# Mixing layer and first two up pairs issued from one list of single steps, residual stores on SyncE's queue, three gates of attention scaled from PSUM

## The chip, the cores and the metric

The kernel runs on one core of one Trainium2 chip. The time is in device microseconds, from runs of the whole program. The core has five engines with a queue each: TensorE (PE in the profile; PEld is its weight load), VectorE (DVE), ScalarE (ACT), GpSimd (POOL) and SyncE (SP). Matrix products go to PSUM, all else lies in SBUF or in device memory.

## What is computed

One decoder layer on 1024 tokens of width 1024, in float32, and a final norm. Cut to what matters here:

```python
xn = rmsnorm(x, norm_mix_w)
da_q, da_k, da_v, sw_q, sw_k, sw_v, g_da, g_sw = split_cols(xn @ w_in)
y_da = diff_attention(da_q, da_k, da_v, lam, lam_init, subln_w)
y_sw = sliding_window_attention(sw_q, sw_k, sw_v, sinks)
merged = sigmoid(g_da) * (y_da @ w_br_da) + sigmoid(g_sw) * (y_sw @ w_br_sw)
x = x + merged @ w_mix_out
xn = rmsnorm(x, norm_ffn_w)
u = xn @ w_up                     # 2 * 2816 columns: gate and value
c = causal_depthwise_conv3(u, conv_w, conv_b)
x = x + (silu(gate(c)) * value(c)) @ w_down
return rmsnorm(x, norm_final_w)
```

## The kernel before

**Layout and products.** Everything lies transposed: channels on the 128 partitions, tokens along the free axis, so a tile holds 128 channels of 1024 tokens, and a half (`hf`) 512 tokens. For precision every operand is split into a high part (a rounded copy, made on ACT) and a low part (what is left, made on DVE by a subtraction), and a product is three matmuls of 512 columns per 128 rows: high by high, high by low, low by high. Large products are done two blocks at a time by Strassen's scheme with seven block products (`P1` to `P7`) instead of eight, on sums and differences of operand halves. In names, `B11`, `B21`, `B22`, `T1`, `T3` (together `T13`), `T2`, `T4` (together `T42`; `N2` is `T2` with its sign turned) are activation operands, `A11`, `A12`, `A22`, `S1` to `S4` weight operands.

**Stages.** `project` makes queries, keys, values and gates; two blocks of columns make a pair (`self.pairs`), the last being the gates 21 and 22. The norm's factor `rstd` (one per token) is multiplied in after a product. A pair's two results `us` are multiplied by it on POOL (line 523); gates are stored to device memory (`gd`, line 525, on SP), the others go through `keep`. `attention` runs six units (four heads of differential attention, two groups of sliding windows). Between its steps `back_half` (line 635) does the products of the gates 23 to 33 by halves, as filler for TensorE, in the order of `HALVES`: ACT copies the half out of PSUM (line 642), unscaled, and ACT's queue stores it (643). The weights, the attention bias and the query and key stacks `u` are loaded on SP's queue.

**Gates before mixing.** `rest` runs over eight pairs of strips `m` in the order 0, 4, 1, 5, 2, 6, 3, 7. For each it loads the gate of both branches (line 878), multiplies it by `rstd` on POOL (line 881) where it was stored unscaled (branch 1 always; branch 0, gates 18 to 25, for m of 5, 6 and 7), takes the sigmoid on ACT (883), and multiplies on DVE with the branch products in PSUM (893, 900, 901). `mix_operands` makes the operands of the mixing layer from two merged strips (932 to 937).

**Mixing layer.** `mix` has 28 runs (`run`, slots 0 to 27), each of twelve matmuls, in two groups of 14 (G = 0 and 14) of two strips each. Two runs share a unit of weights: one load on SP, a cast `wh` on ACT (206) and a low part `wl` on DVE (208), held in two buffers. Runs of one strip accumulate in one PSUM bank; after each the bank is added on DVE to one half of the residual `X[m]` (`add`, line 1032), which frees it for the next run. When a half is complete, `post` takes its square on ACT (994) and adds that on POOL to the sum over channels (995), stores the half to device memory on ACT's queue (`x2d`, line 999), and for m > 3 multiplies it by the norm's weight (`norm_w`, 987) into another tile; for m < 4 that multiply overwrites the half in place, after the store has read it. From the normed strips come the operands of the up products by `cast` (ACT, 1008), `low` (DVE, 1017) and `diff` (DVE, 1024).

**Order.** Each step is entered as an event with a number, `at(16.02, add, ...)`; the events are sorted by it and issued in that order. `in_order` then ties every instruction of ACT, DVE and POOL to the one before it on its engine, so these three run in the listed order. TensorE's and SP's instructions are not tied: their order is made by the framework when the program is built, from the order of issue and its own estimate of when data are ready.

**Up products.** `hidden` does 22 pairs of blocks of `w_up`. Pair 0 is written out: the first three of four strips of five products, then the split of `T42`, then the fourth strip, the column sums (235) and the norm's factor (`power` on POOL, 244), then `P6` and `P4`. Its results are combined on DVE, while pair 1 is prepared: weight sums on POOL (`sums`), casts and low parts. Then the first two products of pair 1 and the `spread` of the factor over the partitions (250). `steady` does the pairs from 1 on.

Of the kernel before, what the change touches and what calls it, by code (L numbers as in the profile page):

```python
# [26 lines left out]
RAW = 3  # L27
HP, HPB, HR = 7, 13, 11
# [13 lines left out]
NVEC = C_LAM + 256  # L42


class Trunk:
# [286 lines left out]
    def project(self):  # L332
# [6 lines left out]
        with ExitStack() as ctx:  # L339
# [171 lines left out]
            for j, ms in enumerate(self.pairs):  # L511
# [10 lines left out]
                for m, u in zip(ms, us):  # L522
                    nc.gpsimd.tensor_tensor(u, u, self.rstd, ALU.mult)  # L523
                    if self.kind[m] == "g":
                        nc.sync.dma_start(self.gd[m - 18], u)
                    else:
                        self.keep(m, u, (tp, "hi"))
# [100 lines left out]
    def store(self, dst, src):  # L628

        self.stores.append((dst, src))  # L630
# [5 lines left out]
    def back_half(self, m, hf):  # L636
# [5 lines left out]
        self.nc.scalar.copy(g, ps)  # L642
# [200 lines left out]
    def rest(self, gctx):  # L843
        nc, tc = self.nc, self.tc
        with ExitStack() as ctx:
            e = ctx.enter_context
            actx, mctx, gctx3 = ExitStack(), ExitStack(), ExitStack()
            with gctx, ExitStack() as bctx:
# [22 lines left out]
                for m in self.mix_order:  # L871
# [4 lines left out]
                    for br in range(2):  # L876
# [3 lines left out]
                        if br or m > 4:  # L880
# [64 lines left out]
    def mix(self, ga, gb, mctx, gctx3):  # L945
# [40 lines left out]
        def norm_w(m, hf):  # L986
            nc.scalar.mul(h2(t42[m - 4] if m > 3 else X[m], hf), h2(X[m], hf), self.vecs[:, C_NF + m:C_NF + m + 1])

        def post(m, hf):

            x = h2(X[m], hf)
            if hf in begun:
                sq = self.tl(stp, [P, H2], "s")
                nc.scalar.activation(sq, x, AF.Square)  # L994
                gt(h2(acc, hf), h2(acc, hf), sq, ALU.add)  # L995
            else:
                nc.scalar.activation(h2(acc, hf), x, AF.Square)
# [5 lines left out]
        events = []  # L1003
        at = lambda p, f, *a, **k: events.append((p, len(events), lambda: f(*a, **k)))
# [14 lines left out]
        def put(p, q, name, k, t):  # L1019
            at(p, cast, name, k, t)  # L1020
            at(q, low, name, k, t)
# [4 lines left out]
        def run(slot, bank, name, first):  # L1026
            if slot % 2 == 0:
                self.unit = self.wq.pop(0)
            self.product(bank(), [t[:, slot % 2 * 4:slot % 2 * 4 + 4] for t in self.unit], name, first=first, skip=True)
# [24 lines left out]
        for G, a in ((0, 0), (14, 2)):  # L1054
            for d in range(2):
# [3 lines left out]
                for slot, n, name, fresh in ((2 * d, n1, "B11", True), (2 * d + 1, n2, "B21", True), (2 * d + 4, n1, "T2", False),  # L1059
                                             (2 * d + 5, n3, "T1", True), (2 * d + 8, n1, "T3", False), (2 * d + 9, n3, "B22", False),  # L1060
                                             (d + 12, n1, "T4", False)):
                    at(G + slot, run, slot, (lambda n=n, x=x: new(n, (n, x))) if fresh else old(n), name, fresh)
                for slot, m, hf, n, sign in ((0, x, 0, n1, ALU.add), (1, x, 0, n2, ALU.add), (4, x, 1, n1, ALU.add), (5, x + 4, 1, n3, ALU.subtract),
                                             (8, x + 4, 1, n1, ALU.subtract), (9, x, 1, n3, ALU.add), (12, x + 4, 0, n1, ALU.subtract)):
                    p = G + slot + (d if slot == 12 else 2 * d) + 1.02
                    at(p, add, m, hf, old(n), sign)
                    if slot in (1, 8, 9, 12):
                        if slot == 8:
                            at(p, tile42, x)
                        at(p + (.28 if p > 28 else .43), post, m, hf)  # L1070
                    if slot == 1:
                        at(p + 1.88, norm_w, x, 0)
                    if slot == 9:
                        at(p + (1.6 if x == 3 else 1.7 if x == 2 else 1.88), norm_w, x, 1)
            for u in range(7):
                if G + 2 * u < 26:
                    at(G + 2 * u + .05, self.ahead, 1)
        at(-.9, load, 0)
        at(-.8, load, 4)
        at(-.7, load, 1)  # L1080
        at(-.6, load, 5)
        at(-.5, load, 2)
        at(13.3, load, 3)
        at(14.3, load, 6)
        at(15.3, load, 7)
        part = lambda *names: lambda: self.mix_operands(3, *names, ga=ga, gb=gb)
        at(-.4, part("B11", "B21"))
        at(.5, part("B22", "T13"))
        at(1.6, part("N2", "T4"))
        put(3.95, 4.4, "B11", 0, xh(0, 0))  # L1090
        put(9.6, 10.1, "B22", 0, th(0, 1))
# [625 lines left out]
```

## Time and profile before

| | us |
|---|---|
| median of three runs | 1336.41 |
| lowest and highest | 1334.08, 1336.58 |
| the profiled execution, its own time | 1336.43 |
| its span, from the first to the last instruction | 1334.5 |

The profile is that of one execution. Times in it count from the first instruction. A view by stretches gives the busy time of each engine between two times, with the clock that TensorE was granted (1.00 is full) and the share of the DMA engines. A list of waits says which instruction of an engine waited for which other, in total, how often and longest. In a timeline a row has start, duration, engine, line of the kernel, operation, output and inputs by the program's names, shapes, count and, in brackets, the idle time before it with what ended it. `n` and `bank` are PSUM banks of the mixing and up products, `g`, `sc` and `t` those of gates, scores and transposes; `m...` and `B_0`, `T_0` are operands, `x` the residual strips, `c` and `t` the strips of `T42`.

### The profile page before, as it was taken

What the parts mean: (1) busy time and instruction counts of PE and PEld (TensorE: products, weight loads), DVE (VectorE), ACT (ScalarE), POOL (GpSimd) and SP (SyncE); (2) the same over time, 40 slices, a digit from 0 to 9 for tenths busy, and PEclk for the clock granted to TensorE, in tenths of its full rate; (3) what the DMA queues carried; (4) which work ended last, traced back from release to release, by engine and by line L of the source; (5) the groups of instructions that cost most, each with busy time, mean ns of one, the idle gap of its engine ahead of it and who ended that gap; (6) DMA issues with size and microseconds to landing.
All of it is one profiled execution on the core that took longest, in us unless ns stands there. A gap on an engine that the chain in (4) does not pass through costs nothing.

```text
span 1334.5 us, 17079 instructions
## 1 busy us (share of the span) xinstructions
PE 1306.9 (98%) x6162; PEld 1085.0 (81%) x6162; DVE 1061.7 (80%) x1458; ACT 670.2 (50%) x1071; POOL 466.0 (35%) x371
## 2 busy tenths in 40 slices
PE   9999999999999999999989999999999999999997
PEld 7888888788888878777777888888888888888886
DVE  8866674288888976986868988888988898896865
ACT  8422232267667766334455454545454544554543
POOL 0448675100111003311226676657666632000002
PEclk9999999999999999999989999999999999999999
DMA  8256786876544236344533537745655249833534
GB/s 290 96 200 168 228 228 193 251 194 175 143 131 139 94 114 243 124 152 157 182 127 119 181 129 177 165 168 127 198 144 125 73 138 311 304 99 116 166 97 146
DMA packets 79332, 220.64 MB, mean 165 GB/s; under 512 B 8848, under 2 KB 16656, under 8 KB 79120
## 3 DMA queue, kind: packets, MB, share of 16 engines
q1 hardware_dynamic: 61760, 186.52, 42.6%
q0 software_dynamic: 4608, 15.73, 7.3%
q10 hardware_dynamic: 12880, 17.31, 3.7%
q8 instruction: 48, 0.79, 0.3%
q14 instruction: 36, 0.29, 0.1%
HBM read 169.72 MB, written 81.26 MB: 188 GB/s over the span
## 4 chain that ended last, share of the span: by engine, by line
PE 77%; DVE 9%; issue 4%; ACT 4%; DMA 3%; POOL 2%; SPq 1%; POOLq 0%; ACTq 0%; DVEq 0%
PE n L1157 30%; PE y L1530 9%; PE t L1157 9%; PE d L1530 7%; PE g L227 3%; PE g L228 3%; PE g L229 3%; PE sc L713 3%; PE t L729 1%; PE t L832 1%; PE sc L801 1%; DVE wl L208 1%; DMA yr<-gd 1%; PE t L741 1%; PE t L822 1%
## 5 line engine op out<-in xcount | busy, mean ns | idle before, releaser
L1460 POOL TENSOR_TENSOR us<-us,rstd 128x1024 f32<-128x1024 f32 x42 | 105.2, 2506 | 146.6 <-DVE us L1374 110.8
L208 DVE TENSOR_TENSOR wl<-raw,wh 128x1024 fp32r<-128x1024 f32 (+2 forms) x91 | 95.4, 1049 | 47.5 <-ACT wh L206 39.2
L206 ACT CAST wh<-raw 128x1024 fp32r<-128x1024 f32 (+2 forms) x91 | 80.4, 884 | 87.1 <-PE y L1530 47.5
L157 DVE TENSOR_TENSOR sl<-sf,sh 128x1024 fp32r<-128x1024 f32 x44 | 107.6, 2447 | 3.9 <-ACT sh L150 3.9
L244 POOL TENSOR_TENSOR rs<-ms,mhalf 128x8 f32<-128x8 f32 (+2 forms) x9 | 13.3, 1474 | 247.4 <-DVE ms L242 241.2
L1386 DVE SCALAR_TENSOR_TENSOR c<-us,vecs,c 128x1024 f32<-128x1024 f32 x76 | 95.6, 1279 | 0.7
L1530 PE MATMUL y<-h,wh 128*128 128x512 f32 (+1 forms) x324 | 95.2, 377 | 0.0
L1530 PE MATMUL d<-h,wh 128*128 128x512 f32 x264 | 81.3, 389 | 0.0
L227 PE MATMUL g<-xh,wh 128*128 128x512 f32 x176 | 71.5, 406 | 1.5 <-ACT g L642 1.5
L228 PE MATMUL g<-xl,wh 128*128 128x512 f32 x176 | 70.8, 402 | 0.0
L229 PE MATMUL g<-xh,wl 128*128 128x512 f32 x176 | 70.8, 402 | 0.0
L1530 PEld LDWEIGHTS y<-h,wh 128*128 128x128 f32 x324 | 59.4, 188 | 11.1
L717 DVE CUSTOM_DVE_ANT_0 L<-sc,bias 128x128 f32<-128x128 f32 (+7 forms) x64 | 47.7, 751 | 21.6 <-PE sc L713 18.4
L718 ACT ACTIVATE L<-L,sm 128x128 f32<-128x128 f32 (+7 forms) x64 | 49.6, 778 | 24.7 <-DVE sm L717 22.0
L1530 PE MATMUL y<-h,wl 128*128 128x512 f32 (+1 forms) x162 | 60.9, 376 | 0.0
L523 POOL TENSOR_TENSOR us<-us,rstd 128x1024 f32<-128x1024 f32 x18 | 52.2, 2905 | 17.3 <-DVE us L546 15.6
L1530 PEld LDWEIGHTS d<-h,wh 128*128 128x128 f32 x264 | 49.6, 188 | 10.3
L995 POOL TENSOR_TENSOR rstd<-rstd,s 128x512 f32<-128x512 f32 x14 | 21.5, 1539 | 91.7 <-ACT s L994 91.7
L713 PE MATMUL sc<-u,u 128*128 128x512 f32 (+2 forms) x192 | 50.0, 360 | 3.2 <-DMA u<-qd 3.0
L696 POOL MEMSET aT<- 128x128 f32 x32 | 6.1, 204 | 132.5 <-PE t L742 96.0
L157 DVE TENSOR_TENSOR wl<-raw,wh 128x1024 fp32r<-128x1024 f32 (+1 forms) x23 | 27.6, 1201 | 30.4 <-ACT wh L150 30.4
L1530 PE MATMUL d<-h,wl 128*128 128x512 f32 x132 | 51.5, 390 | 0.0
(747 smaller groups left out, 4252.0 us busy)
## 6 DMA issues: line engine op xcount, KB each, us to landing
u<-qd SPq DMA_DIRECT2D x72, 256.0 KB, 6.9
raw<-in_w_up SPq DMA_DIRECT2D x24, 512.0 KB, 3.9
raw<-in_w_in SPq DMA_DIRECT2D x22, 512.0 KB, 5.6
rv<-in_w_up SPq DMA_DIRECT2D x22, 512.0 KB, 3.5
hd<-c SPq DMA_DIRECT2D x22, 512.0 KB, 5.4
sdP<-in_w_down POOLq DMA_DIRECT2D x16, 704.0 KB, 8.5
qd<-us SPq DMA_DIRECT2D x15, 512.0 KB, 3.8
raw<-sdP SPq DMA_DIRECT2D x16, 384.0 KB, 3.0
```

What stands on the lines that cost most here:

```text
L157: self.nc.vector.tensor_tensor(lo, src, hi.bitcast(F32), ALU.subtract)
L206: self.hi = nc.scalar.copy(wh, raw)
L208: self.lo = (eng or nc.vector).tensor_tensor(wl, raw, wh.bitcast(F32), ALU.subtract)
L227: nc.tensor.matmul(ps, wh[:, kc + o, :], ah, start=first and n == 0, stop=False)
L228: nc.tensor.matmul(ps, wh[:, kc + o, :], al, start=False, stop=False)
L229: nc.tensor.matmul(ps, wl[:, kc + o, :], ah, start=False, stop=last and n == len(kcs) - 1)
L523: nc.gpsimd.tensor_tensor(u, u, self.rstd, ALU.mult)
L713: nc.tensor.matmul(sc[:, lo + n0:lo + n1], qs, k[c][part][:, n0:n1], start=part == 0, stop=part == 1)
L1157: nc.tensor.matmul(ps, (ah, ah, al)[p][:, k, :], (bh, bl, bh)[p], start=first and n == p == 0, stop=last and p == 2 and n == len(ks) - 1, ...
L1386: nc.vector.scalar_tensor_tensor(c, us[:, 2 - n:T + 2 - n], cw[2 - n], c, ALU.mult, ALU.add)
L1460: i = (nc.vector if m % NF == 0 else nc.gpsimd).tensor_tensor(us[:, 2:], us[:, 2:], self.rstd, ALU.mult)
L1530: nc.tensor.matmul(ps, v[:, k - k0, :], x, start=start and k == i == 0, stop=k == HK - 1 and i == 2, skip_group_check=True)
```

## The change

The sorted events of `mix` and the hand-written start of `hidden` give way to two lists of named steps (`STEPS`), issued in the order in which they stand, again under `in_order`. A name's first letters say what it is: `l` load of a strip of x, `C` and `O` cast and low part of a mixing operand of strip 3, `S` the sums of operand halves between them, `r` a run, `a` an add, `wc` and `wl` cast and low part of a unit of weights, `q` the square, `s` the store, `n` the norm's weight, `c` and `o` cast and low part of an up operand, `d` a difference, `raw` a load of weights, `sa` and `sb` weight sums, `P` products of the up pairs with their part, `sp` and `csp` the spread and the copy of it. What `post` did in one is now three steps, and the store is on SP's queue. The spread comes after the first two products of pair 1, not before the first of them is ready.

Gates 21 and 22 leave `project` unscaled. `LATE` names the gates that are scaled in `rest`: these two (m of 3 and 4 in branch 0) and all of branch 1. The gates 23, 24 and 25 are scaled in `back_half`, on DVE, as they leave PSUM.

```diff
+LATE = (21, 22, *range(26, 34))
+STEPS = (
+    """
+    l5 CB11 OB11 CB21 OB21 S1 banks l4 l0 r0 r1 S2 wc1 wl1 CT13 OT13 r2 l2 CB22 OB22 a0 S3 CN2 a1 r3 wc2 l1 wl2 ON2 S4 a2 a3 s0_0 r4 a4 r5 wc3 wl3 wc4
+    q0_0 n0_0 r6 wl4 r7 wc5 q1_0 r8 a5 a8 s1_0 CT4 wl5 a6 OT4 a7 r9 a9 s0_1 r10 q4_1 q0_1 cB11_0 oB11_0 r11 wc6 wl6 wc7 a10 n0_1 wl7 n4_1 d1_0 cB22_0 r12
+    a11 q5_1 q1_1 oB22_0 s5_1 d2_0 cT13_0 r13 a13 wc8 n1_0 a12 wl8 r14 r15 r16 s1_1 n4_0 cB21_0 n5_0 oT13_0 d3_0 n5_1 s4_1 oB21_0 s5_0 q4_0 q5_0 a14 a15
+    wc9 wl9 cB11_1 oB11_1 n1_1 r17 q2_0 s2_0 d4_0 n2_0 wc10 l3 raw0_sb r18 d1_1 d2_1 cT3_1 wl10 s4_0 cB21_1 a16 a17 oT3_1 cB22_1 oB22_1 d3_1 r19 a18 wc11
+    wl11 r20 a20 cB11_2 l6 r21 cT1_1 q3_0 oB21_1 wc12 d4_1 s3_0 n3_0 cB11_3 r22 oT1_1 oB11_2 l7 a19 a21 a22 q6_1 r23 oB11_3 wl12 n6_1 cB22_2 a23 s2_1 wc13
+    wl13 r24 a24 r25 raw0 q2_1 n2_1 d1_2 q7_1 r26 a25 s7_1 s3_1 d2_2 oB22_2 s6_1 cg_0 og_0 cT13_2 q3_1 a26 oT13_2 n7_1 cB22_3 r27 q6_0 raw0_sa n6_0 cB21_2
+    n3_1 s6_0 a27 n7_0 oB21_2 q7_0 d3_2 oB22_3 s7_0
+    """,
+    """
+    csa_0 cB21_3 osa_0 csb_0 osb_0 d1_3 d4_2 d2_3 cT42_1 oB21_3 d3_3 d4_3 oT42_1 places cT13_3 cT42_3 P1_0 P2_0 cT42_2 P5_0 P7_0 oT13_3 oT42_3 P3_0 cT42_0
+    oT42_0 cv_0 oT42_2 outs P1_1 P2_1 P5_1 P7_1 raw1 P3_1 sums P6_0 mean cg_1 og_1 ov_0 P4_0 results s1 u2 u4 u3 power sa1 csa_1 osa_1 c11 c12 c22 places2
+    sb1 raw2 P1_2 sa2 P2_2 sp0 sp1 csb_1 osb_1 cv_1 ov_1 csp0 csp1 c21
+    """,
+)
...
                 for m, u in zip(ms, us):
-                    nc.gpsimd.tensor_tensor(u, u, self.rstd, ALU.mult)
+                    if m < 21:
+                        nc.gpsimd.tensor_tensor(u, u, self.rstd, ALU.mult)
...
-        self.nc.scalar.copy(g, ps)
+        if m in LATE:
+            self.nc.scalar.copy(g, ps)
+        else:
+            self.nc.vector.tensor_tensor(g, ps, self.rstd[:, hf * H2:(hf + 1) * H2], ALU.mult)
...
-                        if br or m > 4:
+                        if 18 + 8 * br + m in LATE:
                             i = nc.gpsimd.tensor_tensor(g, g, self.rstd, ALU.mult)
...
-            nc.scalar.dma_start(self.x2d[m, :, hf * H2:(hf + 1) * H2], x)
-            if m > 3:
-                norm_w(m, hf)
...
+        def store(m, hf):
+            nc.sync.dma_start(self.x2d[m, :, hf * H2:(hf + 1) * H2], h2(X[m], hf))
...
+        def at(name, f, *a, **k):
+            assert name not in step
+            step[name] = lambda: f(*a, **k)
+
+        def weights():
+            src, nk, *more = self.wsrc.pop(0)
+            raw = more[2] if more else self.load_raw(src, nk)
+            wh, wl = (self.tl(self.wp, [P, nk, P], t, F32R) for t in ("wh", "wl"))
+            nc.scalar.copy(wh, raw)
+            self.wq.append((wh, wl, raw))
+
+        def weights_low():
+            wh, wl, raw = self.wq[-1]
+            tt(wl, raw, wh.bitcast(F32), ALU.subtract)
+            self.ahead(0)
...
+                for m in (x, x + 4):
+                    at(f"l{m}", load, m)
+                    for hf in range(2):
+                        at(f"q{m}_{hf}", square, m, hf)
+                        at(f"s{m}_{hf}", store, m, hf)
+                        at(f"n{m}_{hf}", norm_w, m, hf)
...
         with self.in_order(self.last):
-            gone = False
-            for p, n, f in sorted(events, key=lambda e: e[:2]):
...
+            self.steps(0)
...
+    def steps(self, n):
+        for name in STEPS[n].split():
+            self.step.pop(name)()
...
+                    with self.in_order(self.last):
+                        self.steps(1)
```

More of the change, by code (lines that the diff above doesn't have):

```diff
@@ L1075, in mix @@
[L1075 to L1089, printed above, removed]
@@ new lines, in mix, with banks @@
+        at("raw0", fetch_pair)
+        for key in ("sa", "sb"):
+            at(f"raw0_{key}", fetch_sums, key)
+        for key in ("g", "sa", "sb", "v"):
+            at(f"c{key}_0", self.cast, pair, key)
+            at(f"o{key}_0", self.low, pair, key)
+        def banks():
+            gctx3.close()
+            self.pctx.close()
+            self.first = ExitStack()
+            self.psF = self.first.enter_context(tc.tile_pool(name="psE", bufs=1, space=PSUM, reuse_waits="tile"))
+        at("banks", banks)
@@ L1168, in hidden @@
                      ("P3", "S4", "B22"), ("P6", "S2", "T2"), ("P4", "A22", "T4"))
-            more = self.ends
-            for p, key in ((28.04, "sa"), (28.5, "sb"), (29, "v")):
-                more.append((p, len(more), lambda key=key: self.whole(pair, key)))
-            with self.in_order(self.last):
-                for p, n, f in sorted(more, key=lambda e: e[:2]):
-                    f()
             w0 = pair["w"]
@@ new lines, in hidden @@
+                    x42, tt, v = {}, nc.vector.tensor_tensor, {}
+                    at("places", places)
+                    for n, (name, a, b) in enumerate(prods):
+                        ks = ((0, range(3)), (1, (3,))) if n < 5 else ((0, range(4)),)
+                        for part, k in ks:
+                            at(f"{name}_{part}", lambda name=name, a=a, b=b, k=k, part=part, n=n:
+                               self.product(ps[name], w[a], b, k, first=not part, last=bool(part) or n > 4))
@@ new lines, in hidden @@
+                    for n, (a, b) in enumerate((("A11", "B11"), ("A12", "B21"))):
+                        at(f"P{n + 1}_2", lambda n=n, a=a, b=b: self.product(v["b"][n], st[1]["w"][a], b, skip=True))
+                    for hf in range(2):
+                        at(f"sp{hf}", lambda hf=hf: self.spread(v["sps"][hf], v["rs"], hf * 4))
+                        at(f"csp{hf}", lambda hf=hf: nc.scalar.copy(self.rstd[:, hf * H2:(hf + 1) * H2], v["sps"][hf]))
+                    with self.in_order(self.last):
+                        self.steps(1)
+                        assert not self.step, list(self.step)
```

242 lines of the change are left out of this document (111 added, 131 removed).

## The prediction, made before the run

> **What bounds the kernel now.** I read the page first, for the share of each engine, then the busy time by stretches, which gives the granted clock, then the list of waits of TensorE.
>
> ```profile
> span 1334.5 us, 17079 instructions
> PE 1306.9 (98%) x6162; PEld 1085.0 (81%) x6162; DVE 1061.7 (80%) x1458; ACT 670.2 (50%) x1071; POOL 466.0 (35%) x371
> ```
>
> TensorE is busy for 98% of the span, and the change removes no matmul. So it can only win what TensorE loses between matmuls, or by running some of them slowly. The stretches say where that is; the columns after the length are busy us and instructions of PE, weight load, DVE, ACT and POOL, then the granted clock.
>
> ```profile
> core 0: us, PE busy (x) PEld busy (x) DVE busy (x) ACT busy (x) POOL busy (x), PEclk, DMA share, GB/s
> 800.00:820.00 20.00, 20.00 (x90) 16.56 (x89) 16.70 (x12) 10.42 (x14) 13.33 (x10) 1.00 0.67 158
> 254.00:262.00 8.00, 5.03 (x17) 3.86 (x16) 0.00 (x0) 0.25 (x1) 0.00 (x0) 0.79 1.04 276
> 262.00:480.00 218.00, 216.55 (x1337) 187.34 (x1336) 190.23 (x557) 152.71 (x384) 18.78 (x63) 1.00 0.52 144
> 565.00:573.00 8.00, 5.59 (x24) 3.99 (x23) 7.24 (x10) 2.53 (x3) 2.80 (x1) 1.00 0.44 140
> 606.00:613.00 7.00, 4.78 (x20) 3.27 (x20) 5.00 (x7) 3.71 (x6) 0.00 (x0) 1.00 0.21 74
> 659.00:667.00 8.00, 6.22 (x19) 4.07 (x18) 6.66 (x11) 1.94 (x3) 0.00 (x0) 0.79 0.28 74
> 683.00:700.00 17.00, 13.19 (x47) 10.27 (x46) 11.20 (x15) 11.24 (x15) 2.53 (x2) 0.70 0.26 94
> ```
>
> 800 to 820 is how an undisturbed stage looks: 90 matmuls in 20 us at clock 1.00. The other short stretches hold the losses; three of them also show a clock of 0.70 to 0.79. The waits of TensorE that belong to them (total, times, longest):
>
> ```profile
> PE sc L713 <- DMA u<-qd: 3.0, 1, 3.0
> PE g L227 <- DVE ga L901: 2.4, 2, 1.7
> PE n L1157 <- ACT wh L206: 1.9, 1, 1.9
> PE n L1157 <- ACT mB220h L1008: 1.8, 1, 1.8
> PE n L235 <- POOL rstd L995: 1.8, 1, 1.8
> PE n L1157 <- DVE x L1032: 1.4, 1, 1.4
> PE n L1157 <- DVE wl L208: 0.7, 2, 0.4
> PE n L1157 <- ACT wh L150: 0.8, 1, 0.8
> ```
>
> The first is the start of attention, the second the gates before the mixing layer, the next five the mixing layer and the first up pair, the last the second pair.
>
> What the changed stretch could win at most: its matmuls at full pace against what it takes.
>
> ```profile
> 596.40 0.39 PE L1157 MATMUL n<-mB110h,wh 128*128 128x512 f32 x1
> ...
> 715.67 0.49 PE L1157 MATMUL n<-T_0h,sh 128*128 128x512 f32 x1
> ...
> 727.57 383.88 PE n L1157 x1692
> ...
> 39.80 1.68 PE t L235 x16
> ...
> 709.33 1.03 PE L250 MATMUL n<-ident,rs 128*128 128x128 f32 x8
> ```
>
> The first row is the first mixing product, the second the first matmul after those that the new list orders. In the chain of waits 1692 matmuls took 383.88 us, so 0.227 us each. The stretch has 28 runs, seven products of pair 0 and two of pair 1, twelve matmuls each: 444 × 0.227 = 100.7 us, with 1.7 for the column sums (at full clock) and 1.0 for the spreads 103.4. From 596.4 that ends at 699.8; the trace says 715.7. **15.9 us are lost.** They add up: the five waits are 7.6; the clock takes (1 − 0.79) × 8 + (1 − 0.70) × 17 = 6.8; the remaining 1.5 is slow restarting.
>
> **C, the new order of single steps (−13.8).** Count and kind of the compute steps stay; ACT, DVE and POOL follow the list in order before and after, so a step placed behind a late one is late too. I follow the three lossy places.
>
> ```profile
> 607.89 0.62 ACT L922 CAST mT43h<-g 128x512 fp32r<-128x512 f32 x1 [1.41 <-DVE g L937]
> 608.41 1.04 ACT L206 CAST wh<-raw 128x1024 fp32r<-128x1024 f32 x1
> ...
> 609.75 1.22 DVE L208 TENSOR_TENSOR wl<-raw,wh 128x1024 fp32r<-128x1024 f32 x1
> ...
> 597.93 0.68 DVE L923 TENSOR_TENSOR t<-g,t 128x512 fp32r<-128x512 f32 x1
> ...
> 684.06 0.63 ACT L994 ACTIVATE s<-x 128x512 f32<-128x512 f32 x1 [4.25 <-DVE x L1032]
> ...
> 684.59 0.71 ACT L987 ACTIVATE t<-x,vecs 128x512 f32<-128x512 f32 x1
> ```
>
> Stall at 607: the weights of unit 2 are cast behind the cast of operand T4, which waits for DVE. In the new list `CT4` stands a row later and `wc2` right after `CN2`. From 597.9 DVE has seven half-width steps up to `S3` (7 × 0.68) and two full ones (2 × 1.22), so 605.1; `CN2` 0.62 and `wc2` 1.04 give 606.8. r4 wants them at 596.4 + 48 × 0.227 = 607.3. The low part is there at 608.0, wanted at 607.8: a few tenths late instead of 2.
>
> Stall at 661: the first B22 matmul waits for `a19`, which frees its bank. Before, the steps oT1, oT3, d3, d4 of strip 1 stand between `a18` and it; in the new list oT3 and d3 come earlier. After r20 (596.4 + 21 × 2.72 = 653.5) DVE has a20 and five more up to a19: 6 × 0.68 = 4.1, so 657.6; r23 starts at 596.4 + 23 × 2.72 = 659.0.
>
> Stalls at 686 and 689: operand B21 of strip 2. New list, from the end of r26: a26 0.68, then on ACT n7_1, cB22_3, q6_0, n6_0, cB21_2 = 0.71 + 0.62 + 0.63 + 0.71 + 0.62, so 4.0, which is 1.3 after the end of r27; wanted 15 matmuls = 3.4 after it. Then `csa_0` is tight: a27, n7_0, q7_0, the cast 1.04 and its low part 1.22 end 4.3 after r27, wanted 4.5 after. The column sums come 60 matmuls (13.6 us) after r27, so the last POOL add no longer ends late.
>
> I leave 2.1 us for such tight places and for one slow stretch of clock like that of 659: −15.9 + 2.1. Ends: nothing late (−15.9), or the five waits all there again at full clock (−6.8).
>
> The stores are part of C. They go from ACT's queue to SP's.
>
> ```profile
> ACT x L987 <- DMA x2d<-x: 3.3, 3, 1.4
> ...
> raw<-sm SPq DMA_DIRECT2D x8, 512.0 KB, 3.9
> ...
> x2d<-x ACTq DMA_DIRECT2D x16, 256.0 KB, 2.2
> ```
>
> Before, a norm step that overwrites a half of X waits for the store of it on ACT (3.3 us in all), with the weight casts queued behind. In the new list the norm comes at least four steps of ACT and DVE after the add that the store waits for, more than the 2.2 us to landing. On SP sixteen issues stand among the weight loads, and one waiting for its add holds the loads behind it. A load lands in 3.9 us and is asked for two units, 4 × 2.72 = 10.9 us, ahead: cover of 7 us.
>
> The Trainium skill, "DMA: Bandwidth & Descriptors", section "Issuing engines are not separate DMA queues", speaks against this edit: all issuing engines share the same 16 DMA engines, so moving a DMA saves only issue time. No row contradicts it; by it the move alone would be worth nothing to TensorE and C would rest on the order.
>
> **A, gates 21 and 22 no longer scaled in the last projection pair (−2.4).**
>
> ```profile
> 238.02 0.68 DVE L547 TENSOR_TENSOR us<-u,t 128x512 f32<-128x512 f32 x1
> ...
> 237.17 5.34 SPq L525 DMA_DIRECT2D gd<-us  x2
> ...
> 238.83 3.34 POOL L523 TENSOR_TENSOR us<-us,rstd 128x1024 f32<-128x1024 f32 x1 [1.68 <-issue]
> ```
>
> SP's second gate store waits for POOL's multiply and ends at 242.5; the bias and the q and k loads stand behind it, and TensorE waits 3.0 us for them. Without the multiply the store waits for DVE alone, which ends at 238.7: the loads start 3.8 us earlier, more than the wait. All of it would be 3.0 plus (1 − 0.79) × 8 = 1.7 of clock. But TensorE's order is fixed when the kernel is built; where the scores are placed earlier with their loads, the wait stays. Ends 0 and −4.7; I take the middle.
>
> **A′, six halves of gates 23 to 25 scaled from PSUM (+0.5).** Rows 262 to 480 above: DVE is busy 190 of 218 us, TensorE 217, so TensorE is the bound. An eviction there on ACT, and the same shape from PSUM on DVE:
>
> ```profile
> L642 ACT COPY g<-g x22: 564/585/588, 241.9 to 507.3; 128x512 f32<-128x512 f32 x22
> ...
> L1374 DVE TENSOR_TENSOR us<-n,u 128x512 f32<-128x512 f32 x19 | 13.1, 691 | 10.5 <-PE n L1157 10.5
> ```
>
> Two halves fall before the softmax, where DVE idles; four put 2.8 us on DVE, whose freeing of the bank TensorE needs only two steps later. Ends 0 and +2.8; no gain, since ACT is far from the bound.
>
> **B, POOL in the gates before mixing (−2.1).** Branch 0 of m = 5, 6, 7 loses its multiply, m = 3 and 4 get one, early, where POOL already runs without a break.
>
> ```profile
> 545.83 5.81 POOL L881 TENSOR_TENSOR yr<-yr,rstd 128x1024 f32<-128x1024 f32 x2 [7.50 <-DMA yr<-gd]
> ...
> 549.41 2.78 DVE L932 TENSOR_TENSOR ga<-ga 128x512 f32<-128x512 f32 x1
> ...
> 526.06 0.68 DVE L932 TENSOR_TENSOR ga<-ga 128x512 f32<-128x512 f32 x1
> ```
>
> The same DVE step takes 0.68 beside no POOL work on SBUF and 2.78 behind it. The second multiply of that POOL row is m = 6, branch 0. DVE then has almost no gap until the wait of 2.4 (7.24 of 8 us), so 2.1 us less there is 2.1 less wait. Ends 0 and −3.0 (with restarting).
>
> **D, the second pair (+0.5).** The spreads move behind pair 1's two products, so rstd comes up to 1.0 us later to DVE's scaling, behind which the cast of 0.8 us' wait stands. Ends −0.8 and +1.0.
>
> **Sum**, against the profiled execution's 1336.4 (span 1334.5 and 1.9 around it, equal to the median): −13.8 − 2.4 + 0.5 − 2.1 + 0.5 = −17.3, so **1319.1**. The stages behind carry it through: from 727.57 on the chain is TensorE alone.
>
> **Rivals.**
> - *Nothing left late*: −15.9 − 4.7 − 3.0 − 0.8 = −24.4, 1312. For it: the hand sums fit nearly everywhere. Against: `csa_0` has 0.2 us. 0.12.
> - *New waits in place of old*: C at −6.8, A at 0: −6.8 + 0.5 − 2.1 + 0.5 = −7.9, 1328.5. For it: DVE steps of 0.68 become 2.8 beside POOL, and POOL's fourteen adds fall elsewhere now. 0.18.
> - *The slow clock stays without the waits*: C keeps −7.0, A the middle of 0 and −3.0: −7.0 − 1.5 + 0.5 − 2.1 + 0.5 = −9.6, 1326.8. For it: waits of 1.9 and 2.4 went with clock 1.00, one of 1.4 with 0.79, so the wait is not the whole cause. 0.08. The Trainium skill, "TensorE: Matmul & The Clock Gate", section "Part 1: The HAM clock gate", has the clock halved after an idle window of about 3.4 us; by that rule none of these waits of the mixing layer would halve it, which is this rival. The row with 0.79 disagrees.
> - *SP held up by a store*: from the point where a store stands over 7 us ahead of its add, each of the thirteen weight units can be late by a store's landing: 13 × 2.2 = 28.6, with the rest kept −17.3 + 28.6 = +11.3, 1347.7. Against: most stores stand well behind their add. 0.06.
> - *Given back*: the steady pairs run DVE at 16.7 of 20 us, so a backlog could absorb the gain; within 0.2%. 0.04.
>
> The forecast itself has 0.52. Faster by over 0.2% (2.7 us, about what a measurement of this kernel can tell from no change): 0.52 + 0.12 + 0.18 + 0.08 = 0.90; same 0.04; slower 0.06. The range takes in the first four cases: 1311.5 to 1329.
>
> **What would show it.** The stretch from the first mixing product to the first T_0h product of pair 1 should last 103 to 107 us, not 119, at clock 1.00; u<-qd under 2 us among TensorE's waits; ga L901 gone; L881 ten times, not eleven. I am wrong if new waits of n L1157 sum to over 5 us, or SP's raw loads land late behind x2d stores.

## The result, and the profile after

The changed kernel takes **1318.6 us** (median of 4 executions, 1317.45 to 1319.94), the kernel before 1336.06 beside it: a ratio of 0.9872, 95% interval 0.9855 to 0.9889. The forecast was 1319.1. A second set of four executions of the changed kernel (e9 below) gave 1319.28, 0.988 of before (0.9866 to 0.9895).

The helper lines have moved: L1157 is now L1185 (mixing and up products), L227 is L246, L642 is L663 with the new L665 beside it, L881 is L904, L901 is L924, L987 is L1012, L208 is L1042 in the mixing layer. The head of the page first, span and TensorE:

```profile
span 1316.6 us, 17069 instructions
PE 1300.2 (99%) x6162; PEld 1080.8 (82%) x6162; DVE 1057.2 (80%) x1464; ACT 666.7 (51%) x1065; POOL 457.3 (35%) x368
```

Then the busy time by stretches of the kernel before: attention from the first score product to the last product with V, the gates from the first branch product to the first mixing product, and the stretch that the new list orders, from the first mixing product to the first T_0h product of pair 1. The columns are those of the prediction.

```profile
257.28:491.38 234.10, 231.78 (x1400) 199.00 (x1401) 199.73 (x582) 159.78 (x404) 18.99 (x65) 0.99 0.53 146
506.36:596.40 90.04, 87.63 (x386) 71.92 (x384) 74.43 (x79) 39.30 (x47) 29.08 (x11) 1.00 0.45 153
596.40:715.67 119.27, 111.46 (x469) 89.25 (x468) 89.15 (x105) 59.08 (x82) 33.16 (x21) 0.94 0.44 153
```

The same three of the changed kernel:

```profile
254.27:489.66 235.39, 231.13 (x1401) 197.39 (x1400) 202.23 (x586) 158.13 (x401) 17.97 (x65) 1.00 0.53 145
504.63:591.67 87.04, 87.04 (x386) 72.07 (x384) 71.43 (x79) 38.58 (x47) 27.20 (x10) 1.00 0.45 158
591.67:697.88 106.21, 104.84 (x469) 85.25 (x467) 87.04 (x105) 58.61 (x82) 32.87 (x21) 1.00 0.53 172
```

Read the first two numbers of each row. The 17.9 us of the span come from four places: the first score product 3.0 earlier (257.28 to 254.27), the gates 3.0 shorter and without a gap on TensorE (87.04 of 87.04 busy), the ordered stretch **13.1** shorter. Attention gives 1.3 back. What follows the stretch is unchanged within 0.1. The clock, before 0.99 in attention and 0.94 in the ordered stretch, is 1.00 in all three.

TensorE's waits in the changed kernel (total, times, longest), without three of 1.5, 1.1 and 0.8 that are as before; what has to be compared with the list in the prediction is which of those names are still there:

```profile
PE g L246 <- ACT g L663: 2.5, 4, 0.8
PE t L855 <- DVE aT L849: 1.3, 1, 1.3
PE n L1185 <- ACT wh L169: 0.6, 1, 0.6
PE n L1185 <- DVE x L1071: 0.5, 1, 0.5
PE n L1185 <- DVE sl L176: 0.5, 1, 0.5
PE n L1185 <- ACT sh L169: 0.3, 1, 0.3
```

The waits for u<-qd (3.0) and for ga (2.4) are gone, and of the five large ones of mixing four; the one for the add (DVE x) has gone from 1.4 to 0.5. In the stretch 1.3 us are left (the last three rows; the third row of the list is pair 2's). The first two rows have grown, both in the second half of attention: 2.5 and 1.3, against 1.5 and 0.4 before.

### The profile page after: what moved, and what is told of

Same layout as the page of the kernel before. It is cut to its first block, busy times and chain, and to the rows that moved or that the text cites. A ratio compares the mean times of both kernels' runs of the same rounds, so it can differ in the third digit from the quotient of the medians.

```text
span 1316.6 us, 17069 instructions
## 1 busy us (share of the span) xinstructions
PE 1300.2 (99%) x6162; PEld 1080.8 (82%) x6162; DVE 1057.2 (80%) x1464; ACT 666.7 (51%) x1065; POOL 457.3 (35%) x368
## 5 line engine op out<-in xcount | busy, mean ns | idle before, releaser
L1509 POOL TENSOR_TENSOR us<-us,rstd 128x1024 f32<-128x1024 f32 x42 | 105.2, 2506 | 146.8 <-DVE us L1423 111.0
L225 ACT CAST wh<-raw 128x768 fp32r<-128x768 f32 (+2 forms) x78 | 66.9, 859 | 89.0 <-PE y L1579 50.7
L227 DVE TENSOR_TENSOR wl<-raw,wh 128x768 fp32r<-128x768 f32 (+2 forms) x78 | 79.6, 1022 | 31.9 <-ACT wh L225 31.8
L263 POOL TENSOR_TENSOR rs<-ms,mhalf 128x8 f32<-128x8 f32 (+2 forms) x8 | 11.6, 1452 | 237.1 <-DVE ms L261 234.2
L246 PE MATMUL g<-xh,wh 128*128 128x512 f32 x176 | 70.8, 402 | 2.5 <-ACT g L663 2.5
L1579 PEld LDWEIGHTS d<-h,wh 128*128 128x128 f32 x264 | 49.6, 188 | 10.2
L169 ACT CAST sh<-sf 128x1024 fp32r<-128x1024 f32 x44 | 46.3, 1052 | 10.2 <-POOL sf L155 6.2
L543 POOL TENSOR_TENSOR us<-us,rstd 128x1024 f32<-128x1024 f32 x16 | 46.5, 2911 | 8.3 <-DVE us L566 8.2
```

Of the source, the lines that this page charges most:

```text
L225: self.hi = nc.scalar.copy(wh, raw)
L227: self.lo = (eng or nc.vector).tensor_tensor(wl, raw, wh.bitcast(F32), ALU.subtract)
L246: nc.tensor.matmul(ps, wh[:, kc + o, :], ah, start=first and n == 0, stop=False)
L1509: i = (nc.vector if m % NF == 0 else nc.gpsimd).tensor_tensor(us[:, 2:], us[:, 2:], self.rstd, ALU.mult)
L1579: nc.tensor.matmul(ps, v[:, k - k0, :], x, start=start and k == i == 0, stop=k == HK - 1 and i == 2, skip_group_check=True)
```

## The experiments

Twelve runs, each of four executions (e4 of five, e5 of twelve), one of them profiled. Stages are those of the rows above, from the profiles; the median is that of the executions; in the expectations the gates end with the start of their last product, 0.2 us sooner. The kernel before stood at 1335.98 beside e1 to e4, at 1336.01 beside e5 to e8 and at 1334.62 beside e9 to e12.

| run | edit | median us | first score at | attention | gates | stretch |
|---|---|---|---|---|---|---|
| before | | 1336.06 | 257.3 | 234.1 | 90.0 | 119.3 |
| changed | | 1318.60 | 254.3 | 235.4 | 87.0 | 106.2 |
| e1 | changed, gates 21 and 22 on POOL early | 1321.22 | 256.7 | 236.2 | 87.0 | 106.5 |
| e2 | changed, nothing scaled from PSUM | 1319.92 | 253.7 | 232.5 | 91.9 | 106.4 |
| e3 | changed, stores on ACT | 1323.10 | 253.9 | 236.1 | 87.0 | 112.0 |
| e4 | before, all gate edits | 1331.24 | 253.7 | 235.1 | 87.0 | 117.1 |
| e5 | before, stores on SP | 1335.53 | 256.9 | 234.2 | 89.3 | 119.9 |
| e6 | changed, wc2 behind T4 | 1321.14 | 253.3 | 237.0 | 87.0 | 108.4 |
| e7 | changed, a19 two steps later | 1319.26 | 253.6 | 236.2 | 87.0 | 106.8 |
| e8 | changed, gate 25 on POOL late | 1318.54 | 255.1 | 232.2 | 90.1 | 106.6 |
| e9 | changed, once more | 1319.28 | 253.7 | 236.5 | 87.0 | 106.5 |
| e10 | changed, a19 and sa earlier | 1320.14 | 254.8 | 235.5 | 87.0 | 107.3 |
| e11 | changed, gate 25 on DVE late | 1316.69 | 256.3 | 233.1 | 87.1 | 106.3 |
| e12 | e10 and e11 | 1316.41 | 254.0 | 233.0 | 87.0 | 107.1 |

### e1: part A undone

```diff
-LATE = (21, 22, *range(26, 34))
+LATE = tuple(range(26, 34))
...
-                    if m < 21:
-                        nc.gpsimd.tensor_tensor(u, u, self.rstd, ALU.mult)
+                    nc.gpsimd.tensor_tensor(u, u, self.rstd, ALU.mult)
```

> The changed kernel, but gates 21 and 22 are again multiplied on POOL in the last projection pair, before they are stored (part A undone; the multiply of both is then missing where they are loaded, so nothing is done twice). Theory: in the changed kernel the loads of q and k start 4 us earlier and TensorE's wait for them (3.0, with 1.7 of half clock) went as a whole; attention behind it gave back 2.4 us for a reason that lies elsewhere (the six gate halves on DVE). Then this kernel has the u<-qd wait of about 3.0 us back, the first score product comes at 257.3 instead of 254.3, and the time is 4.2 us longer, 1322.8. Rival: attention is paced by its own softmax steps and absorbs what comes early; then the wait is back too, but the last attention product comes only 1.7 us later than in the changed kernel and the time is 1320.3. The forecast's own middle value was 2.4.

1321.22, 0.9893 of before (0.9876 to 0.9909): 1.9 to 2.6 above the two sets of the changed kernel, between theory and rival. First the waits of e1, one row; then its clock around that wait, in the columns of the stretches:

```profile
PE sc L735 <- DMA u<-qd: 2.6, 1, 2.6
```

```profile
253.00:260.00 7.00, 4.44 (x20) 3.42 (x19) 0.69 (x1) 0.00 (x0) 0.00 (x0) 1.00 1.02 258
```

The wait is back with nearly its old length, so A is what removed it. The half clock that followed the same wait before did **not** come back in this profile (1.00): the wait alone doesn't bring it, see the last section. Of e1's four executions one has a lower clock (0.995, the others 0.998) and took 1324.96, 3.3 to 4.5 more than the rest; it was not profiled, so where it lost that isn't known. Attention absorbed nothing (236.2, against 235.4 and 236.5). A is worth the wait, about 2.5.

### e2: A' and B undone

```diff
-LATE = (21, 22, *range(26, 34))
+LATE = tuple(range(21, 34))
```

> The changed kernel, but gates 23, 24 and 25 are again copied by ACT and multiplied later by POOL, thirteen multiplies there instead of ten (A' and B undone, A kept). Theory: the six halves on DVE are what attention lost; from first score to last attention product it takes 2.4 us less than in the changed kernel (235.8 to about 233.4), and the gates before the mixing layer lose 3.0 again to waits for POOL: together 1319.2, within 1 us of the changed kernel. Rival: the loss in attention is that of the fixed order of TensorE's instructions and has nothing to do with DVE; then attention stays at 235.8, only the 3.0 come back, 1321.6.

1319.92, 0.9879 (0.9866 to 0.9893). Its waits:

```profile
PE g L246 <- DVE ga L924: 3.8, 3, 2.2
PE g L246 <- ACT g L663: 1.5, 4, 0.5
```

The numbers are the theory's, only larger: attention 232.5, 2.9 to 4.0 shorter than the changed kernel's two profiles, and the gates 4.8 longer. With thirteen multiplies TensorE waits for ga again, three times. So A' cost as much as the forecast's upper end or more, and B won a little more than that: together they are worth about 1 us. That the loss is DVE's load, as the theory has it, this run doesn't show, since TensorE's order changed with it (e8).

### e3 and e5: the stores, in the new and in the old order

```diff
 e3, changed kernel
-            nc.sync.dma_start(self.x2d[m, :, hf * H2:(hf + 1) * H2], h2(X[m], hf))
+            nc.scalar.dma_start(self.x2d[m, :, hf * H2:(hf + 1) * H2], h2(X[m], hf))
 e5, kernel before
-            nc.scalar.dma_start(self.x2d[m, :, hf * H2:(hf + 1) * H2], x)
+            nc.sync.dma_start(self.x2d[m, :, hf * H2:(hf + 1) * H2], x)
```

> The changed kernel, with the sixteen stores of the residual stream on ACT's queue again, at the same places of the list. Theory: the order does the work, and the queue is nearly free: the stretch from the first mixing product to the first T_0h product of pair 1 stays between 106 and 107.5 us (106.2 in the changed kernel), the time between 1318 and 1320. Rival: a store that waits for its add on ACT's queue holds the weight casts behind it, as ACT's waits before the change suggest: new waits of n L1185 for ACT wh of over 2 us in all, the stretch 109 us or more, 1322 or more. Third: the stores land earlier on ACT (2.2 us against 2.8), and ACT's 6.4 us of waits for them shrink; then the time goes down by up to 1 us.

> The kernel before, with the sixteen stores of the residual stream issued on SP's queue instead of ACT's; the old order by due times, the old gates. In the new order the queue was worth 5.8 us of the stretch from the first mixing product to the first T_0h product of pair 1 (112.0 with the stores on ACT, 106.2 on SP). Theory: what a store does on ACT's queue, holding the casts behind it until its add is done, it does in the old order too; then the stretch goes from 119.3 to about 114, and the time to 1331. Rival: the queue and the order go together; in the old order the late casts are late for DVE's sake, the five waits stay, and a norm step waits longer for a store that now lands later: the stretch stays between 117.5 and 121, the time between 1334 and 1338.

In both cases the times are the rival's. e3: 1323.10, 0.99 (0.9886 to 0.9913), the stretch 5.8 longer than the changed kernel's. The waits are not the ones that the rival named: `ACT wh` has 0.5, not over 2. The third theory, shorter waits of ACT for the stores, fell: 7.3 against 6.4. The instructions of ACT in e3 show what the stores do there (start, duration, what it waited for):

```profile
652.98 0.33 ACTq L1025 DMA_DIRECT2D x2d<-x  x1
656.45 0.72 ACT L1012 ACTIVATE x<-x,vecs 128x512 f32<-128x512 f32 x1 [2.44 <-DMA x2d<-x]
...
661.45 0.33 ACTq L1025 DMA_DIRECT2D x2d<-x  x1
661.87 1.05 ACT L1037 CAST wh<-raw 128x1024 fp32r<-128x1024 f32 x1 [2.24 <-DVE x L1071]
```

The first two in the changed kernel:

```profile
646.93 0.32 SPq L1025 DMA_DIRECT2D x2d<-x  x1
652.85 0.72 ACT L1012 ACTIVATE x<-x,vecs 128x512 f32<-128x512 f32 x1
```

Two things happen. A store is issued only when ACT's order gets to it: this one, the tenth of the sixteen, 6 us later than on SP. So it lands late, and the norm step that overwrites the half stands 2.44 for it, where it waited for nothing in the changed kernel. And from 659.6 ACT has nothing to do but stands at the next store, which waits for its add on DVE; the weight cast behind it is 2.2 late. TensorE's rows in e3:

```profile
660.87 0.50 PE L1185 MATMUL n<-mT130h,wl 128*128 128x512 f32 x1 [1.42 <-DVE wl L1042]
675.83 0.50 PE L1185 MATMUL n<-mB220l,wh 128*128 128x512 f32 x1 [0.66 <-DVE mB220l L1056]
```

The larger wait ends before the store of 661.45 is issued, so it comes from the landing: behind the norm step stand the cast of the operand, its low part on DVE and then the low part of the weights that TensorE waits for. In all TensorE waits 3.5 in the stretch of e3 and 1.3 in that of the changed kernel. Most of the rest of the 5.8 is half clock, which the changed kernel doesn't have there:

```profile
678.87:685.70 6.83, 6.83 (x23) 5.86 (x23) 6.80 (x10) 3.50 (x4) 0.00 (x0) 0.50 0.20 78
```

6.8 us at half clock cost up to 3.4. All four executions of e3 have a mean clock of 0.996, those of the changed kernel 0.997 and 0.998.

e5: 1335.53, 1.0004 of before (0.9992 to 1.0015), nothing. Its waits of TensorE in mixing, where the stores have left ACT and the casts are as late as ever:

```profile
PE n L1157 <- ACT mB220h L1008: 2.0, 1, 2.0
PE n L1157 <- DVE wl L208: 2.0, 1, 2.0
PE n L1157 <- ACT wh L206: 1.9, 1, 1.9
PE n L235 <- POOL rstd L995: 1.8, 1, 1.8
```

With the stretch as measure the four corners are 119.3 (old order, ACT), 119.9 (old, SP), 112.0 (new, ACT) and 106.2 (new, SP). The two of the old order have the old gates; with the new ones e4 below has 117.1. So the order alone gives 5 to 7, the queue alone nothing, and on top of the order it is worth 5.8. Half clock lies in the first three of the corners (13.7, 10.2 and 6.8 us of it). The gaps between TensorE's matmuls alone, length less busy time, say the same: 7.8, 9.3, 3.5 and 1.4. The new list has its stores where ACT cannot afford to stand.

### e4: the gates alone, in the kernel before

The edit is that of the gates in the change, all three places, without the new list.

> The kernel before, with the change of the gates alone (A, A' and B; old order, stores on ACT's queue). Theory: the parts add up: A -4.2, A' +2.4, B -3.0, so -4.8 against before, 1331.3, and the stretch from the first mixing product to the first T_0h product of pair 1 keeps its 119.3 us with the same waits. Rival: the stages pay for each other (the waits in the mixing layer follow from when POOL and DVE come free in the gates): then the stretch changes by over 2 us, either way. By the forecast's own terms it would be -4.0, 1332.1.

1331.24, 0.9965 (0.9952 to 0.9979), 4.7 less than before: the theory's 4.8. Its attention and gates are those of the changed kernel (235.1 and 87.0). The stretch became 2.2 shorter, though, which was the rival's bound; its waits of mixing are the old ones (2.0, 2.0, 1.9 and 0.9), and its half clock lasts 6.8 us there, against 3.4 and 10.2 before. 6.8 us less at half clock are worth up to 3.4, more than the 2.2, so nothing shows that the stages pay for each other. The profiled execution was also the fastest of the five, 1329.13, 2.1 under the median; the sum is the theory's by the median, not by this profile.

### e6 and e7: two places of the list put back

```diff
 e6
-S3 CN2 a1 r3 wc2 l1 wl2 ON2 S4 a2 ... s1_0 CT4 wl5 a6 OT4 a7
+S3 CN2 a1 r3 l1 ON2 S4 CT4 wc2 OT4 wl2 a2 ... s1_0 wl5 a6 a7
 e7
-oB11_2 l7 a19 a21 a22 q6_1
+oB11_2 l7 a21 a22 a19 q6_1
```

> The changed kernel with one place of the list as it was: the cast of operand T4 again ahead of the cast of weight unit 2. Theory (the forecast's first place): the cast of T4 waits for the fourth sum on DVE, unit 2 comes about 2 us late for the fifth product of strip 0, with a wait of n L1185 for ACT wh of 1.5 to 2.2 and the stretch 2.0 to 2.5 longer, about 108.4; the clock stays at 1.00, since the wait leaves the 3.41 us window of the clock over a third busy, so the time is 1320.8. Rival: in the new list the weights have slack elsewhere and the place is not what counted; the stretch stays within 0.5 of 106.2.

1321.14, 0.9896 (0.9881 to 0.9911). TensorE's rows at the place:

```profile
604.28 0.50 PE L1185 MATMUL n<-mN20h,wh 128*128 128x512 f32 x1 [0.80 <-ACT wh L1037]
...
605.54 0.50 PE L1185 MATMUL n<-mN20h,wl 128*128 128x512 f32 x1 [0.30 <-DVE wl L1042]
```

The place is the one forecast, the stretch 108.4 as expected and the time 1.9 to 2.5 more than the changed kernel's; the two waits are smaller than expected (0.8 and 0.3). Counted from start to start of the matmuls, which takes in the slow start behind a wait, the place costs 1.6, and a wait for an add at 649 another 0.6. The clock stayed at 1.00.

> The changed kernel with the add a19 two steps later, behind a21 and a22, which wait for later products. Theory (the forecast's second place): a19 frees the bank that the third product of pair 0's B22 needs; a22 waits for the end of r22, so a19 ends about 1.7 us after it, where it is 0.5 late in the changed kernel; the wait of n L1185 for DVE x at about 654 grows from 0.5 to 1.6 or so, the stretch from 106.2 to 107.4, and the time by 1.1, to 1319.7; no half clock, as the window keeps over a third of activity. Rival (each wait of 1.4 us or more is followed by 3.4 us of half clock, as the one at 661 before the change): 1.7 more, a stretch of 109.1.

1319.26, 0.9888 (0.987 to 0.9905), the stretch 106.8: no difference from the changed kernel that could be told, and half of what the theory expected. The first B22 product does start later (656.7, where the changed kernel has 655.2), but the order of TensorE's instructions, made anew at the build, has put four matmuls of other products ahead of it, 0.9 us of work. Why a19 is late at all is seen on DVE in the changed kernel, with POOL beside it:

```profile
649.35 2.11 DVE L1042 TENSOR_TENSOR wl<-raw,wh 128x1024 fp32r<-128x1024 f32 x1
...
654.51 1.88 DVE L1071 TENSOR_TENSOR x<-x,n 128x512 f32<-128x512 f32 x3
656.90 1.22 DVE L1042 TENSOR_TENSOR wl<-raw,wh 128x1024 fp32r<-128x1024 f32 x1
```

```profile
649.09 1.29 POOL L1019 TENSOR_TENSOR rstd<-rstd,s 128x512 f32<-128x512 f32 x1 [7.99 <-ACT s L1018]
657.18 2.10 POOL L1019 TENSOR_TENSOR rstd<-rstd,s 128x512 f32<-128x512 f32 x1 [6.80 <-ACT s L1018]
```

The low part of the weights took 2.11 us where a POOL add had begun 0.3 before it, and 1.22 seven us later, where POOL's add began 0.3 after it and took 2.10 instead of 1.29 itself: the step that starts second is the one that loses. That 0.9 is more than all of the wait (0.5). a19 is the first of the three adds in the row in the middle.

### e8 and e11: gate 25

```diff
 e8
-LATE = (21, 22, *range(26, 34))
+LATE = (21, 22, *range(25, 34))
 e11, with the same line, and
-                            i = nc.gpsimd.tensor_tensor(g, g, self.rstd, ALU.mult)
+                            i = (nc.gpsimd if br or m < 7 else nc.vector).tensor_tensor(g, g, self.rstd, ALU.mult)
+                            if m == 7 and not br:
+                                tc.add_manual_dep(i.ins, self.hi.ins.name, ..., reason="late")
```

> The changed kernel with gate 25 alone copied by ACT and multiplied later on POOL; gates 23 and 24 still scaled from PSUM by DVE. The order of TensorE's instructions in attention is then, instruction by instruction, that of the run without any scaling from PSUM. Theory: the 2.9 us that attention lost (235.4 against 232.5) come with gate 25, whose two halves lie within the softmax steps; here attention takes 232.5 to 233, and the gates before the mixing layer stay at 86.8, as the eleventh multiply falls at about 520, where POOL already runs: 1315.7 to 1316.5, less than the changed kernel. Rival: the six halves cost alike, so 4 of 6 of the loss stays: attention 234.4, 1317.6. Second rival: an eleventh multiply is one too many for the gates, whose waits for ga come back with 1 to 3 us: 1317 to 1319.

1318.54, 0.9879 (0.9863 to 0.9895). Half of the theory holds: attention is back at 232.2 although gates 23 and 24 are still scaled on DVE. The second rival holds as well: the eleventh multiply brings waits for ga of 2.1 back, the gates take 90.1, and the sum is nought. TensorE near the end of attention, the changed kernel first, then e8:

```profile
481.98 1.03 PE L845 MATMUL t<-ident,L 128*128 128x128 f32 x8
484.30 1.20 PE L855 MATMUL t<-aT,v 128*128 128x512 f32 x4 [1.29 <-DVE aT L849]
```

```profile
479.50 1.14 PE L845 MATMUL t<-ident,L 128*128 128x128 f32 x8
480.39 0.47 PE L248 MATMUL g<-xh,wl 128*128 128x512 f32 x1
...
481.17 0.40 PE L248 MATMUL g<-xh,wl 128*128 128x512 f32 x1
481.93 1.20 PE L855 MATMUL t<-aT,v 128*128 128x512 f32 x4 [0.37 <-DVE aT L849]
```

In e8 four gate matmuls stand between the transposes and the product that needs them, and cover all but 0.4 of the way through DVE; in the changed kernel none is left there. The order is written down when the kernel is built: by the matmuls' names and shapes it is in attention one and the same in the six kernels with gate 25 on ACT (before, e2, e5, e8, e11, e12), and another, the same again, in the eight with gate 25 on DVE. This place lies 200 us behind gate 25's two halves (at 266 and 288), which speaks for the order as the cause, and not for DVE's load; a kernel with the one and not the other was not tried. The gaps of TensorE in attention add up to 4.3 in the changed kernel and 2.1 in e8; the third microsecond of the loss lies in the busy time (231.1 against 230.0) and was not placed.

> The changed kernel with gate 25 copied by ACT in attention, and multiplied at the end of the gates stage on DVE, after the operand casts of strip 2, where DVE idled 1.8 us; ten multiplies on POOL as in the changed kernel. TensorE's order in attention is that of the run with gate 25 on POOL. Theory: both parts keep their best: attention 232.2 to 232.5 and the gates 86.8 to 87.3, so about 3 us less than the changed kernel, 1315.6. Rival: the multiply (1.2) and the sigmoid behind it (1.1) are late for the last gate product and so for the first mixing product: gates 88 or more, 1317 or more.

1316.69, 0.9861 (0.9846 to 0.9875), 2.6 less than the changed kernel beside it (1319.28), 1.9 less than its first set: the theory, with attention 233.1 and the gates 87.1. (The profile is of its slowest execution, 1318.32; there the full clock was granted 10.9 us after the start, in the changed kernel's 7.7. Until then matmuls start every 0.43 us, then every 0.23, so it is 1.4 late early on, which is most of its late first score, 256.3.) DVE at the end of the gates:

```profile
584.25 1.22 DVE L904 TENSOR_TENSOR g<-g,rstd 128x1024 f32<-128x1024 f32 x1
586.60 1.22 DVE L918 TENSOR_TENSOR g<-g,sc 128x1024 f32<-128x1024 f32 x1 [1.12 <-ACT g L908]
588.92 0.70 DVE L939 TENSOR_TENSOR g<-yr,g 128x512 f32<-128x512 f32 x1 [1.11 <-PE g L248]
```

The multiply and the sigmoid behind it fit ahead of the next step, which still waits 1.1 for TensorE.

### e9, e10 and e12: the changed kernel again, and two late steps moved

```diff
 e10
-cB11_3 r22 oT1_1 oB11_2 l7 a19 a21 a22
+cB11_3 r22 a19 oT1_1 oB11_2 l7 a21 a22
...
-cB21_2 n3_1 s6_0 a27 n7_0 ... csa_0 cB21_3 osa_0 csb_0
+cB21_2 s6_0 a27 n7_0 ... csa_0 osa_0 n3_1 cB21_3 csb_0
```

> The changed kernel itself, beside the three that follow, on one chip. 1318.6 again, within 0.8; the stretch from the first mixing product to the first T_0h product of pair 1 within 0.5 of 106.2, the gates 86.8, attention from first score to last product between 235.4 and 237.0, as the three runs with the same attention show it (the start of attention moves by up to 1 us with the phase of the clock's window).

All as expected: 1319.28, stretch 106.5, attention 236.5.

> The changed kernel with three steps of the list moved: a19 ahead of the low parts of T1 and B11 (two steps of 0.68 on DVE), and the norm of the second half of tile 3 behind the split of the sum operand sa, whose cast so comes 0.7 us earlier on ACT. Theory: the three waits left in the stretch, 0.64 at 655, 0.47 at 673 and 0.63 at 675, were each late by a step or two on DVE or ACT and go: the stretch 106.2 - 1.7 = 104.5, the time 1316.9. Rival: ACT and DVE are both without gaps there, and what is moved back is late in its turn (the last cast of B21, or the low part of T1): the sum of the waits stays, the stretch stays between 105.7 and 106.7.

1320.14, 0.9887 (0.9871 to 0.9904), 0.9 more than e9: the rival's kind of end, and a little beyond its bound, 107.3. The wait at 655 went, but those for sa grew from 0.3 and 0.5 to 0.4 and 1.1. DVE ahead of the low part of sa (its row has two steps), and POOL's last add, in e10:

```profile
673.65 1.77 DVE L1056 TENSOR_TENSOR mN22l<-x,mN22h 128x512 fp32r<-128x512 f32 x1
675.34 2.35 DVE L176 TENSOR_TENSOR sl<-sf,sh 128x1024 fp32r<-128x1024 f32 x2
```

```profile
673.43 1.44 POOL L1019 TENSOR_TENSOR rstd<-rstd,s 128x512 f32<-128x512 f32 x1 [0.86 <-ACT s L1018]
```

and the same DVE step in the changed kernel, with ACT ten us sooner:

```profile
672.47 0.68 DVE L1056 TENSOR_TENSOR mN22l<-x,mN22h 128x512 fp32r<-128x512 f32 x1
```

```profile
662.86 0.72 ACT L1012 ACTIVATE x<-x,vecs 128x512 f32<-128x512 f32 x1 [3.01 <-DMA x2d<-x]
```

The move brought POOL's add from 0.2 behind the start of a DVE step to 0.2 ahead of it, and the step, which took 0.68, now takes 1.77; the low part of sa is 1.1 late for it, more than the 0.7 won on ACT. The last row is one reason why ACT is short of time there: a norm step that overwrites half a tile of X stands 3.0 us for a store of it that hasn't landed. Moving that store was not tried.

> The last two together. Theory: they lie in different stages and add up: 1318.6 - 1.7 - 3.0 = 1313.9. Rival: one of them fails, and the sum is that of the other, 1315.6 or 1316.9.

1316.41, 0.9858 (0.9844 to 0.9873): the rival, e11's gain without one from e10. It is the lowest of all, 2.9 under e9, though not to be told from e11.

## Why the prediction was right, and where it was not

**What bounds the kernel** held: only gaps and slow clock were won, and with TensorE busy for 99% few are left.

**C** was forecast at −13.8 and measured −13.1 in the stretch; clock 1.00, 106.2 within the 103 to 107 that were to show it. By places: the stall at 607 went, and e6 gives it back, 1.6 of it at the place; those at 686 and 689 went; at 661 the sum had a19 end 1.4 us ahead of need, but it counted 0.68 and 1.22 for DVE and not the 2.11 beside POOL, so 0.5 of wait stayed; `csa_0`, named as tight, is late by 0.3 with 0.5 behind it. The allowance for a slow clock wasn't needed. One sentence of C fell: that the norm comes late enough for the store to have landed. ACT's waits for stores rose:

```profile
ACT x L1012 <- DMA x2d<-x: 6.4, 2, 3.4
```

against 3.3 before, with a landing of 2.8 us instead of 2.2. The longer landing goes with the order and not with the queue, as the rows of the changed kernel, e3 and e5 show (the last number is the median landing):

```profile
x2d<-x SPq DMA_DIRECT2D x16, 256.0 KB, 2.8
x2d<-x ACTq DMA_DIRECT2D x16, 256.0 KB, 3.5
x2d<-x SPq DMA_DIRECT2D x16, 256.0 KB, 2.1
```

So the expectations of e3 (stores land earlier on ACT) and e5 (later on SP) had that the wrong way round. And the queue was weighed too lightly. By the Trainium skill, "DMA: Bandwidth & Descriptors", section "Issuing engines are not separate DMA queues", the move alone saves only the time of issuing, and C would have rested on the order. The first half is so (e5), the second not: 5.8 of the 13.1 need the stores off ACT (e3). What counted was not the price of an issue but when the engine gets to it, and what stands behind it.

**A**: −2.4 forecast, −1.9 to −2.6 by e1. The wait went as a whole, so the fixed order did not keep it. The 1.7 of half clock that made the lower end −4.7 went too, but in e1's profile it stayed away with the wait there, so it can't be put down to A with certainty.

**A'** is the term that failed: +0.5 forecast, about +3 measured (attention 235.1 to 237.0 in eight profiles with gate 25 on DVE; 232.2 to 233.1 in four without; before and e5, also without, have 234.1 and 234.2 with 3.4 us of half clock in them), at and beyond its end of +2.8. That DVE had room was right, as e8 shows for gates 23 and 24. The step that failed is the one that let TensorE's freeing of the bank come two steps later and counted nothing else: TensorE's order in attention was made anew with it, and the new one waits. That it is the order and not DVE's load is argued (e8), not shown by a run with the one alone.

**B**: −2.1 forecast, −3.0 measured, its end: the wait for ga is gone, ten multiplies instead of eleven. e8 and e2 show how near the edge the gates are: eleven cost 3.0, thirteen 4.8.

**D**: +0.5 forecast, −0.1 measured.

So the sum came out within a microsecond partly because errors cancelled: A' was put 2.5 too low, C 0.7 too low, B 0.9 and D 0.6 too high, and with the wait at the start of attention 1.5 us of half clock went that no term counted in full. That the sum is so close is in part luck.

**The rivals.** Something stayed late, so it was not 1312; the waits that are left in the stretch are 1.3 us, so it was not 1328.5; the slow clock went. Stores did hold SP up: all sixteen waited there for their adds, 30.2 us in all and 6.4 at the longest, so the argument that most stand well behind their add was wrong. But 6.4 is under the 7 us of cover: one weight load came 0.8 late for DVE, and TensorE waited for none. e3 shows that mechanism on the other queue.

## What to carry to other kernels

A queue and an order are one edit: a store on a compute engine's queue costs the wait for its data at the place where it stands, and it is issued, and lands, no sooner than that engine gets to it; whether that matters is read from the steps behind it. When a step moves to another engine, look whether the static order of the engine that bounds changes with it; a stage can lose more there than the step costs. Price a two-input DVE step by whether a POOL step has begun before it (2.11 here) or not (1.22), above all in a hand-written list without slack.

## What the hardware showed that was not expected

The half clock depends on where a wait falls, and not on its length alone. The clock records show only full and half clock. Apart from the one at the program's end, the half-clock stretches last 3.413 us or a multiple of it, and they start at multiples of 3.413 us from each other within a run: before, the starts 256.97, 663.16 and 687.05 are 119 and 7 such windows apart. The same wait of 1.9 for the weights of unit 2, at the same instruction, in the window that it falls into; before, then e4, then e5, there with the next one:

```profile
608.52:611.94 3.42, 2.13 (x8) 1.47 (x9) 3.30 (x5) 1.58 (x3) 0.00 (x0) 1.00 0.20 78
```

```profile
602.63:606.04 3.41, 1.82 (x7) 1.21 (x8) 3.02 (x4) 1.86 (x3) 0.00 (x0) 1.00 0.20 77
```

```profile
605.91:609.33 3.42, 1.48 (x7) 0.86 (x6) 2.68 (x5) 2.03 (x3) 0.00 (x0) 1.00 0.00 0
609.33:612.74 3.41, 3.29 (x8) 2.15 (x7) 1.92 (x3) 1.98 (x4) 0.00 (x0) 0.50 0.63 216
```

With TensorE busy for 2.13 or 1.82 of a window the clock stays; with 1.48 the next window runs at 0.50. Busy time is no exact measure, since the ends of matmuls are modelled and a tiny one counts for much: two windows with the column sums were followed by half clock at 2.14 (e3) and 2.22 (e5). An estimate by columns does better. Count 0.227 us for a matmul of 512 columns, as the prediction measured it, and less in proportion for a smaller one. Then, in all fourteen profiles, every window of full clock with up to 0.97 us of work was followed by half clock, every one from 1.43 up by full, and between the two both occur. So the bound lies near a third of a window, as the expectations of e6 and e7 had it. The Trainium skill, "TensorE: Matmul & The Clock Gate", section "Part 1: The HAM clock gate", has a free-running window of 3413 ns, which these starts bear out, but gives an idle window of about 3.4 us as the condition; here windows with up to 1.42 us of work in them were enough. Each window of half clock costs up to 1.7 us, and whether a wait meets one is partly chance: e5 has much the same waits in mixing as before, and three half-clock stretches there (10.2 us) instead of two (13.7 us); e1 has the wait of 2.6, split over two windows of 2.25 and 2.02 us busy, and no half clock.
